# Three stretches of a two-block fp32 network on one Trainium2 core: job order in a recurrent layer, queries and heads in an attention, and a closing norm in columns

## The chip, the cores and the metric

One Trainium2 chip, one core. The metric is the device time of one execution in microseconds (us); the time of a kernel is the median of its runs.

## What is computed

512 tokens of width 1024 go through two layers, then through a third block of another kind and a last norm. Everything is float32. The parts that the change touches, cut from the reference:

```python
def rms_norm(x, g):
    return x * lax.rsqrt(jnp.mean(x * x, axis=-1, keepdims=True) + EPS) * g

def rglru_mixer(h, w_in, conv_w, conv_b, w_a, b_a, w_x, b_x, lam, w_out):   # layer 0
    gate, xr = jnp.split(h @ w_in, 2, axis=-1)
    gate = jax.nn.gelu(gate)
    xc = causal_conv4(xr, conv_w, conv_b)
    r = sigmoid(blockwise(xc, w_a) + b_a)          # 4 blocks of 256
    i = sigmoid(blockwise(xc, w_x) + b_x)
    log_a = -RG_C * r * softplus(-lam)
    u = jnp.sqrt(-jnp.expm1(2 * log_a)) * (i * xc)
    hs = scan(h_t = exp(log_a_t) * h_(t-1) + u_t)
    return (hs * gate) @ w_out

def dsa_mixer(h, w_in, kv_norm_g, w_uk, w_uv, w_o, rel_bias):               # layer 1
    q, c, qi, ki, wi = split(h @ w_in)             # 16 heads of 64, latent 128, 8 index heads
    c = rms_norm(c, kv_norm_g)
    q_lat = einsum('bshd,hdc->bshc', q, w_uk) * ATT_SCALE
    score = einsum('bqh,bqhs->bqs', wi, relu(qi . ki))     # index score, causal
    keep the 256 keys of the highest score for each query
    p = softmax(q_lat . c + rel_bias[t5_bucket(dist)])     # over the kept keys
    o = einsum('bshc,hcv->bshv', p . c, w_uv)
    return o @ w_o

x = x + mixer(rms_norm(x)); x = x + mlp(rms_norm(x))       # each layer
return rms_norm(x, norm_final)                             # after the last block
```

## The kernel before

**Layout and precision.** Activations lie transposed: features on the 128 partitions, the 512 tokens along a row, so a vector of width 1024 is 8 tiles of 128x512. A float32 product is made of three rounded (fp32r) products: both operands are split in a high and a low part, and `group` (lines 349 to 351) issues high by high, high by low and low by high into one PSUM bank. A high part is a copy on ScalarE (`h`, line 362; `wh` for weights, line 252), a low part a subtraction on VectorE (`l`, line 363) or, for weights of some layers, on POOL (`wl`, line 253). Weights come in chunks of 512 KB by SP's DMA queue (`wst`, line 246) in the order of `weight_plan`, with four buffers, three chunks ahead; the copies between tiles stand in the same queue. PSUM has 8 banks, which the pool gives out to one product after the other.

**What sets the order.** The work is written as jobs, lists of stages. `run` pipelines them in software: it starts a job's first stage and then takes a later stage of each of the jobs before it. Every engine works off its queue in order. A scheduler fixes each engine's order once, from the recorded order and priorities.

**Layer 0.** Eight `conv_job`s (projection `xr`, convolution `xc`, lines 541 and 544), four `recur_job`s (weights `ax`; gates `rg` and `ig`, lines 568 and 569; scan, line 598) for 256 features each, and eight `rgate_job`s (projection `rgate`, GELU). The order stands in lines 644 to 651: two projections a step, a recurrence job after each of the steps 2 to 5, and after step 4 `bias_job` (lines 622 to 640): a small product of the 32-row bias table with a one-hot matrix, copied out of PSUM by VectorE (`biasrow`, line 639) and stored to DRAM for the attention. Then come the output projections (`rout`, lines 666 to 668).

**Attention.** `index_job` makes the scores (lines 779 to 798). `select` (lines 811 to 814) finds the 256 best keys: per block of 128 queries 16 rounds of MAX8 and MATCH_REPLACE on VectorE, then the mask; the rounds are handed out in the last stages of `q_job` (four each) and of the first heads (two each). `q_job` projects two heads' queries. `kt_job` makes keys and copies halves of them across partitions by DMA (line 849), `v_job` makes values (lines 870 and 873). For each two heads and each half of the tokens ("pair" 0 and 1), `copies` (line 890) brings the queries into a doubled layout by four DMAs of 64 KB (`qd`), and `queries` rounds the copy: `qph` on ScalarE (line 895), `qpl` on POOL (line 896). `head_job` runs 32 times: bias tile by DMA (line 911), logits (lines 927 to 929), softmax (lines 938 to 946, the last step `probs` on POOL), transposes of the probabilities (line 958), their rounding (`pTh` on ScalarE, line 961, `pTl` on VectorE, line 962), values (lines 978 and 979). The last key block of 128 columns is copied unrounded (`pTf`, line 966) and multiplied in one fp32 product (line 981). After every second head the halves are added (`olo`, lines 985 to 988) and rounded (`oh`, `ol`, lines 993 and 994). The order is lines 1003 to 1022: all projections, then keys, then the first four heads among the values, then the others. Then the output projection `wo`.

**Closing norm.** The last four projections are made in two halves of 256 tokens (`last_job`: residual sum line 1453, square line 1429 or 1427, sum of squares line 1433, weighted output `fin` line 1439). `norm_job` (lines 1460 to 1478) takes the total over features by a product with a matrix of ones, which gives it in all 128 partitions (`tot`, line 1467), then root (1471) and reciprocal (1472) of 128x256, the product with `fin` (1477) and the store (1478). The left half's is put into the job list by line 1514.

Of the kernel before, what the change touches and what calls it, by code (L numbers as in the profile page):

```python
# [222 lines left out]
class Weights:  # L223
# [56 lines left out]
def build(ctx, tc, xT, wall, par, relb, onehot, edges, out):  # L280
# [390 lines left out]
    run([residual_job(j, lambda j=j: rout(j), nxt) for j in range(KD)])  # L671
# [146 lines left out]
    def q_job(j):  # L818
# [60 lines left out]
    QD, QP = {}, {}  # L879
# [4 lines left out]
    def copies(pair, j):  # L884

        t = QD[pair, j] = T(name="qd")
        for f in range(2):
            src = QF[j][64 * f:64 * f + 64, 256 * pair:256 * pair + 256]
            for o in (0, 64):
                nc.sync.dma_start(t[o:o + 64, 256 * f:256 * f + 256], src)  # L890

    def queries(pair, j):
        t = QD.pop((pair, j))
        qh, ql = QP[pair, j] = T(F32R, "qph"), T(F32R, "qpl")
        act(qh, t, AF.Copy)
        G.tensor_sub(ql, t, qh.bitcast(F32))
# [6 lines left out]
    def head_job(pair, h):  # L903
# [44 lines left out]
        def transpose():  # L948
            probs = st["p"]
            st["pT"] = []  # L950
            for k0 in range(0, nfull + 1, 2):
# [7 lines left out]
                nf = 256 if k0 + 1 == nfull else 512  # L959
# [3 lines left out]
                pf = None  # L963
                if nf == 256:
                    pf = T(name="pTf")
                    act(pf[:, :P], ps[:, 256:256 + P], AF.Copy)
                st["pT"].append((ph, pl, pf))

        def values():
# [4 lines left out]
            for kt in range(nfull + 1):  # L974
                ph, pl, pf = st["pT"][kt // 2]
                if kt < nfull:
                    c = slice((kt % 2) * 256, (kt % 2) * 256 + 256)
                    PE.matmul(osl, value(kt, h), ph[:, c], start=kt == 0, stop=False)
                    PE.matmul(osl, value(kt, h), pl[:, c], start=False, stop=False)
                else:  # L980
                    PE.matmul(osl[:, P:], value(kt, h).bitcast(F32), pf[:, :P], start=False, stop=True)
# [568 lines left out]
```

## Time and profile before

| | us |
|---|---|
| median of 3 runs | 1905.25 |
| lowest and highest run | 1904.38, 1905.49 |
| the profiled execution, own time | 1903.61 |
| its span, first to last instruction | 1901.8 |
| TensorE busy | 1848.7 (97%) |
| VectorE busy | 1020.3 (54%) |
| ScalarE busy | 813.4 (43%) |
| POOL busy | 181.7 (10%) |

Times in the rows further down are those of the profiled execution, counted from the start of its span. The engines are named PE (TensorE), PEld (its weight loads), DVE (VectorE), ACT (ScalarE), POOL and SPq (SyncE's DMA queue). Matmuls are pipelined and their ends are modelled; the distance between two starts tells what one costs. "PEclk" is the granted clock of TensorE as a share of its full 2.4 GHz, a mean over the stretch; its other level is 1.2 GHz.

### The profile page before, as it was taken

How to read it: one execution, taken by the hardware profiler on the slowest of the kernel's cores; microseconds unless marked ns; L12 is line 12 of the kernel's file. 1: busy time of each engine (PE TensorE's matmuls, PEld its weight loads, DVE VectorE, ACT ScalarE, POOL GpSimd, SP SyncE). 2: the span in 40 equal slices, each digit the busy share in tenths (PEclk: the TensorE clock that was granted, in tenths of full speed). 3: DMA queues.
4: the chain of work that ended last, by engine and by line, in shares of the span. 5: the costliest groups of instructions: out<-in, count | busy, mean ns of one | idle time of the engine just before them, and what ended most of it. 6: DMA issues, size and time to landing. Idle time of an engine off the chain costs nothing.

```text
span 1901.8 us, 21845 instructions
## 1 busy us (share of the span) xinstructions
PE 1848.7 (97%) x8434; PEld 1526.0 (80%) x8434; DVE 1020.3 (54%) x1512; ACT 813.4 (43%) x1271; POOL 181.7 (10%) x194
## 2 busy tenths in 40 slices
PE   8989999999999679999999999999999999999997
PEld 6868888888878468888888888888888888888886
DVE  7886543344349956654244445735584554344345
ACT  6784432333244577443234445446543333132223
POOL 0000000000155264000000014211000000000000
PEclk9999999999999899999999999999999999999998
DMA  5222222222222530322222222231122222222221
GB/s 197 84 86 92 100 98 91 100 100 96 93 100 90 146 89 21 111 93 96 100 100 92 97 100 86 92 111 45 67 89 100 100 89 100 100 95 94 100 80 53
DMA packets 61000, 179.36 MB, mean 94 GB/s; under 512 B 7696, under 2 KB 18144, under 8 KB 60896
## 3 DMA queue, kind: packets, MB, share of 16 engines
q1 hardware_dynamic: 60752, 177.97, 27.6%
q8 instruction: 66, 1.08, 0.2%
q14 instruction: 38, 0.31, 0.0%
q10 hardware_dynamic: 144, 0.00, 0.0%
HBM read 168.48 MB, written 2.12 MB: 90 GB/s over the span
## 4 chain that ended last, share of the span: by engine, by line
PE 63%; DVE 4%; ACT 2%; issue 1%; DMA 0%; POOL 0%; SPq 0%; DVEq 0%; ACTq 0%
PE ps L349 14%; PE ps L351 13%; PE ps L350 13%; PE dn L350 5%; PE dn L351 5%; PE dn L349 5%; PE o L1319 1%; DVE score L812 1%; PE v L1225 1%; PE v L1224 1%; PE v L1226 1%; DVE top L811 1%; ACT probs L941 1%; PE kv L1293 1%; PE tot L376 0%
## 5 line engine op out<-in xcount | busy, mean ns | idle before, releaser
L252 ACT ACTIVATE wh<-wst 128x1024 fp32r<-128x1024 f32 (+2 forms) x314 | 328.2, 1047 | 910.3 <-PE ps L350 358.7
L349 PE MATMUL ps<-xh,wh 128*128 128x512 f32 x1376 | 542.5, 394 | 6.4 <-DVE biasrow L639 4.6
L351 PE MATMUL ps<-xh,wl 128*128 128x512 f32 x1376 | 536.6, 390 | 0.0
L350 PE MATMUL ps<-xl,wh 128*128 128x512 f32 x1376 | 536.5, 390 | 0.0
L253 DVE TENSOR_TENSOR wl<-wst,wh 128x1024 fp32r<-128x1024 f32 (+2 forms) x291 | 352.4, 1212 | 224.3 <-ACT wh L252 197.2
L349 PEld LDWEIGHTS ps<-xh,wh 128*128 128x128 f32 x1376 | 259.3, 188 | 62.8 <-issue 7.2
L350 PEld LDWEIGHTS ps<-xl,wh 128*128 128x128 f32 x1376 | 259.3, 188 | 56.3 <-issue 2.4
L351 PEld LDWEIGHTS ps<-xh,wl 128*128 128x128 f32 x1376 | 259.1, 188 | 54.1
L349 PE MATMUL dn<-h,wh 128*128 128x512 f32 (+1 forms) x712 | 271.7, 382 | 0.0
L350 PE MATMUL dn<-l,wh 128*128 128x512 f32 (+1 forms) x712 | 271.7, 382 | 0.0
L351 PE MATMUL dn<-h,wl 128*128 128x512 f32 (+1 forms) x712 | 271.7, 382 | 0.0
L350 PEld LDWEIGHTS dn<-l,wh 128*128 128x128 f32 x712 | 133.8, 188 | 26.0
L349 PEld LDWEIGHTS dn<-h,wh 128*128 128x128 f32 x712 | 133.8, 188 | 26.0
L351 PEld LDWEIGHTS dn<-h,wl 128*128 128x128 f32 x712 | 133.8, 188 | 25.8
L253 POOL TENSOR_TENSOR wl<-wst,wh 128x1024 fp32r<-128x1024 f32 x23 | 55.2, 2405 | 934.7 <-ACT wh L252 934.5
L422 DVE TENSOR_TENSOR x<-x,dn 128x512 f32<-128x512 f32 x48 | 33.0, 687 | 170.8 <-PE dn L351 170.8
L453 DVE SCALAR_TENSOR_TENSOR relu<-ps,std 128x512 f32<-128x512 f32 x64 | 44.2, 691 | 146.7 <-PE ps L351 146.6
L349 PE MATMUL ps<-h,wh 128*128 128x512 f32 x200 | 78.7, 396 | 5.5 <-ACT h L362 3.5
L350 PE MATMUL ps<-l,wh 128*128 128x512 f32 x200 | 77.8, 389 | 0.0
L351 PE MATMUL ps<-h,wl 128*128 128x512 f32 x200 | 77.8, 389 | 0.0
L349 PEld LDWEIGHTS ps<-h,wh 128*128 128x128 f32 x200 | 37.9, 190 | 15.1 <-ACT h L362 4.0
L1497 DVE TENSOR_TENSOR u<-ps,std 128x512 f32<-128x512 f32 x22 | 15.2, 690 | 62.5 <-PE ps L351 62.5
(315 smaller groups left out, 2129.2 us busy)
## 6 DMA issues: line engine op xcount, KB each, us to landing
wst<-wall SPq DMA_DIRECT2D x300, 512.0 KB, 3.2
btile<-biasdram SPq DMA_DIRECT2D x32, 128.0 KB, 3.0
qd<-qq SPq DMA_DIRECT2D x64, 64.0 KB, 2.1
wst<-wall SPq DMA_DIRECT2D x8, 384.0 KB, 3.0
x<-xT SPq DMA_DIRECT2D x8, 256.0 KB, 4.9
out_dram<-fin SPq DMA_DIRECT2D x8, 256.0 KB, 2.3
wst<-wall SPq DMA_DIRECT2D x6, 256.0 KB, 5.0
kto<-kth SPq DMA_DIRECT2D x8, 128.0 KB, 2.7
```

The source lines that it names most:

```text
L252: self.nc.scalar.activation(h[:, a:b], st[:, a:b], AF.Copy)
L253: eng.tensor_sub(l[:, a:b], st[:, a:b], h[:, a:b].bitcast(F32))
L349: PE.matmul(ps, wh, xh, start=i == 0, stop=False)
L350: PE.matmul(ps, wh, xl, start=False, stop=False)
L351: PE.matmul(ps, wl, xh, start=False, stop=i == n - 1)
L422: V.tensor_add(xs[j], xs[j], st["ps"])
L453: stt(t, st["ps"], 0.0, feed.r, op0=ALU.max, op1=ALU.mult)
L811: V.max(top, acc[:, :w])
L812: V.match_replace(acc[:, :w], top, acc[:, :w], MARK)
L941: act(s[:, :w], s[:, :w], AF.Exp, scale=-1.0, bias=nm, accum_out=sums[:, a:a + 1])
L1224: PE.matmul(st["ps"][i], xh, hk, start=kt == 0, stop=False)
L1225: PE.matmul(st["ps"][i], xh, lk, start=False, stop=False)
```

## The change

- **Layer 0.** A written list, `LAYER0`, sets the order of the jobs and of the weights: the first recurrence job comes after seven convolutions instead of six, the others among the gate projections. `bias_job` moves from there to the middle of the output projections.
- **Queries.** Each projection's queries are rounded once, whole (`qh` on ScalarE, `ql` on POOL), and both rounded tiles are copied: eight DMAs of 64 KB for two heads and a half, where there were four; the roundings of the copies go. The copies are issued four heads ahead.
- **Order of the attention.** Heads 0 to 7 stand among the last two query projections, the keys 2 to 7 and the values. In the weight plan `uk` and `uv` move ahead of the last two query projections.
- **Weights `wo`.** Their low parts are made on POOL.
- **Values.** The last key block is rounded like the others (`pTh`, `pTl` of 384 columns) and multiplied in two fp32r products; `pTf` goes. `olo` is one copy of 128x512, and the sums go to a tile `os`.
- **Closing norm.** The squares are the weights of the product and one column of ones the moving side, so that the total stands as columns, 128x2; root and reciprocal work on these, and two products with the identity spread the columns over 128x256 in PSUM. The left half's norm starts one job earlier.

```diff
+LAYER0 = ([("xr", j) for j in range(7)] + [("ax", 0), ("xr", 7), ("ax", 1), ("rgate", 0), ("rgate", 1), ("ax", 2)]
+          + [("rgate", 2), ("rgate", 3), ("ax", 3)] + [("rgate", j) for j in range(4, 8)])
 def weight_plan():
-    for step in range(8):
-        plan += [("xr" if step < 4 else "rgate", 2 * step % 8 + i) for i in range(2)]
-        if 2 <= step <= 5:
-            plan += [("ax", step - 2)]
+    plan = list(LAYER0)
-    plan += [("att", j) for j in (0, 1, 2, 3, 4, 6, 7, 8, 9, 5, 10, 11, 12, 13)] + [("uk",), ("uv",)]
+    plan += [("att", j) for j in (0, 1, 2, 3, 4, 6, 7, 8, 9, 5, 10, 11)] + [("uk",), ("uv",), ("att", 12), ("att", 13)]
...
-        eng = self.nc.gpsimd if key[0] in ("att", "uk", "uv", "lr", "k", "dec") or key == ("q", 0) else self.nc.vector
+        eng = self.nc.gpsimd if key[0] in ("att", "uk", "uv", "wo", "lr", "k", "dec") or key == ("q", 0) else self.nc.vector
...
-    for step in range(8):
-        jobs += [(conv_job if step < 4 else rgate_job)(2 * step % 8 + i) for i in range(2)]
-        if 2 <= step <= 5:
-            jobs.append(recur_job(step - 2))
-        if step == 4:
-            jobs.append(bias_job())
+    jobs += [{"xr": conv_job, "ax": recur_job, "rgate": rgate_job}[n](j) for n, j in LAYER0]
...
-    run([residual_job(j, lambda j=j: rout(j), nxt) for j in range(KD)])
+    jobs = [residual_job(j, lambda j=j: rout(j), nxt) for j in range(KD)]
+    run(jobs[:4] + [bias_job()] + jobs[4:])
...
         def ev():
-            t = QF[j] = T(name="qq")
+            t = T(name="qq")
             stt(reverse(t), blocks(st["ps"]), 0.125, blocks(feed.r), op0=ALU.mult, op1=ALU.mult)
+            h, l = QF[j] = T(F32R, "qh"), T(F32R, "ql")
+            act(h, t, AF.Copy)
+            G.tensor_sub(l, t, h.bitcast(F32))
...
     def copies(pair, j):
-        t = QD[pair, j] = T(name="qd")
-        for f in range(2):
-            src = QF[j][64 * f:64 * f + 64, 256 * pair:256 * pair + 256]
-            for o in (0, 64):
-                nc.sync.dma_start(t[o:o + 64, 256 * f:256 * f + 256], src)
-    def queries(pair, j):
-        t = QD.pop((pair, j))
-        qh, ql = QP[pair, j] = T(F32R, "qph"), T(F32R, "qpl")
-        act(qh, t, AF.Copy)
-        G.tensor_sub(ql, t, qh.bitcast(F32))
+        QP[pair, j] = []
+        for src, name in zip(QF[j], ("qph", "qpl")):
+            t = T(F32R, name)
+            for f in range(2):
+                for o in (0, 64):
+                    nc.sync.dma_start(t[o:o + 64, 256 * f:256 * f + 256].bitcast(F32),
+                                      src[64 * f:64 * f + 64, 256 * pair:256 * pair + 256].bitcast(F32))
+            QP[pair, j].append(t)
...
-            n = 8 * pair + j
-            if e == 0 and 1 <= n < 14:
-                copies((n + 2) // 8, (n + 2) % 8)
-            if e == 1 and 1 <= n < 15:
-                queries((n + 1) // 8, (n + 1) % 8)
+            n = 8 * pair + j + 2
+            if e == 0 and n < 16:
+                copies(n // 8, n % 8)
...
-                nf = 256 if k0 + 1 == nfull else 512
+                nf = 384 if k0 + 1 == nfull else 512
...
-                pf = None
-                if nf == 256:
-                    pf = T(name="pTf")
-                    act(pf[:, :P], ps[:, 256:256 + P], AF.Copy)
-                st["pT"].append((ph, pl, pf))
+                st["pT"].append((ph, pl))
...
-                    PE.matmul(osl[:, P:], value(kt, h).bitcast(F32), pf[:, :P], start=False, stop=True)
+                dst = osl if kt < nfull else osl[:, P:]
+                PE.matmul(dst, value(kt, h), ph[:, c], start=kt == 0, stop=False)
+                PE.matmul(dst, value(kt, h), pl[:, c], start=False, stop=kt == nfull)
...
-            act(lo[0:64, :256], ops[64:128, 0:256], AF.Copy)
-            act(lo[64:128, :256], ops[0:64, 256:512], AF.Copy)
+            act(lo, ops, AF.Copy)
+            os_ = T(name="os")
-            V.tensor_add(reverse(lo[0:64, 256:512]), blocks(lo[0:64, :256]), blocks(ops[0:64, 0:256]))
+            V.tensor_add(reverse(os_[0:64, :256]), blocks(lo[64:128, 0:256]), blocks(ops[0:64, 0:256]))
...
-    for j in range(1, 8):
+    for j in range(1, 6):
         jobs.append(q_job(j))
+        if j in (4, 5):
+            jobs.append([lambda: None, lambda j=j: copies(0, j - 4)])
...
-    first = []
-    for i in range(4):
-        first += [heads[i], vals[2 * i], vals[2 * i + 1]]
-    run(jobs + [kt_job(j) for j in range(8)] + first + heads[4:])
+    kts = [kt_job(j) for j in range(8)]
+    jobs += kts[:2] + vals[:2] + [heads[0], q_job(6), heads[1], q_job(7)]
+    for i in range(2, 8):
+        jobs += [heads[i], kts[i], vals[i]]
+    run(jobs + heads[8:])
...
         def tot():
-            ps = st["ps"] = PS("tot")[:, :w]
-            for i in range(2):
-                PE.matmul(ps, ones, acc2[i][:, c], start=i == 0, stop=i == 1)
+            ps = st["ps"] = PS("tot")
+            for n in range(w // P):
+                cols = slice(c.start + n * P, c.start + (n + 1) * P)
+                for i in range(2):
+                    PE.matmul(ps[:, n:n + 1], acc2[i][:, cols], ones[:, 0:1], start=i == 0, stop=i == 1)
         def rstd():
-            r = st["r"] = T(name="std")[:, :w]
-            act(r, st["ps"], AF.Sqrt, scale=1.0 / D, bias=eps_t)
-            V.reciprocal(r, r)
+            col = small(w // P, "rstd")
+            act(col, st["ps"][:, :w // P], AF.Sqrt, scale=1.0 / D, bias=eps_t)
+            V.reciprocal(col, col)
+            st["r"] = PS("r")[:, :w]
+            for n in range(w // P):
+                PE.matmul(st["r"][:, n * P:(n + 1) * P], col[:, n:n + 1].to_broadcast([P, P]), ident, start=True, stop=True)
...
-    jobs.insert(-2, norm_left[:3])
+    jobs.insert(-3, norm_left[:3])
```

What moves on the engines, at three places.

**TensorE in layer 0**, where the high part of the first convolved tile (`h_460`) meets the gate weights of the first recurrence job, in four banks. `ps_435` is the bank of the projection `xr` 5, `ps_530` that of `xr` 6. Before:

```order
L349 MATMUL ps_435<-xh_188,wh_308 128x512
L350 MATMUL ps_435<-xl_189,wh_308 128x512
L351 MATMUL ps_435<-xh_188,wl_309 128x512
L349 MATMUL ps_485<-h_460,wh_340 128x512
L349 MATMUL ps_492<-h_460,wh_340 128x512
L349 MATMUL ps_499<-h_460,wh_340 128x512
L349 MATMUL ps_506<-h_460,wh_340 128x512
L349 MATMUL ps_530<-xh_148,wh_382 128x512
```

Of the change (line numbers one higher; `ps_485` is `xr` 6 here, `ps_572` is `xr` 7):

```order
L350 MATMUL ps_485<-xh_188,wh_340 128x512
L351 MATMUL ps_485<-xl_189,wh_340 128x512
L352 MATMUL ps_485<-xh_188,wl_341 128x512
L350 MATMUL ps_527<-h_460,wh_382 128x512
L350 MATMUL ps_534<-h_460,wh_382 128x512
L350 MATMUL ps_541<-h_460,wh_382 128x512
L350 MATMUL ps_548<-h_460,wh_382 128x512
L350 MATMUL ps_572<-xh_148,wh_430 128x512
```

The same products have moved behind one more projection of 24 matmuls.

**VectorE in the selection**, around the end of the rounds for the second block (384 columns): `wl` are low parts of `wo` chunks, `ktl` and `vv` belong to keys and values, L812 and L811 (L809 and L808 of the change) are the rounds, L814 (L811) the mask. Before:

```order
L826 SCALAR_TENSOR_TENSOR qq<-ps,std 128x4x128
L811 MAX top<-score 128x8 x2
L253 TENSOR_TENSOR wl<-wst,wh 128x1024
L812 MATCH_REPLACE score<-top,score 128x384
L846 TENSOR_TENSOR ktl<-ps,kth 128x512
L812 MATCH_REPLACE score<-top,score 128x512
L846 TENSOR_TENSOR ktl<-ps,kth 128x512 x3
L814 TENSOR_SCALAR mask_3774<-score 128x384
L846 TENSOR_TENSOR ktl<-ps,kth 128x512
L811 MAX top<-score 128x8
L253 TENSOR_TENSOR wl<-wst,wh 128x1024
```

Of the change:

```order
L795 TENSOR_TENSOR score<-score,tri 128x128
L808 MAX top<-score 128x8
L873 TENSOR_TENSOR vv<-ps,vv 128x2x128 x2
L809 MATCH_REPLACE score<-top,score 128x384
L808 MAX top<-score 128x8
L809 MATCH_REPLACE score<-top,score 128x384
L808 MAX top<-score 128x8 x2
L809 MATCH_REPLACE score<-top,score 128x384
L809 MATCH_REPLACE score<-top,score 128x512
L811 TENSOR_SCALAR mask_3774<-score 128x384
L873 TENSOR_TENSOR vv<-ps,vv 128x2x128 x2
```

The `wl` rows are gone from VectorE, the `ktl` rows of the keys 2 to 7 stand further down, and `vv` rows stand here. In front of the last mask there are four `wl`, one `ktl` and four `vv` fewer than before.

**VectorE at the end**, from the last rows of the left half's norm on. Before:

```order
L1433 TENSOR_TENSOR sq<-sq 128x256
L1472 RECIPROCAL std<-std 128x256
L1453 TENSOR_TENSOR x<-x,dn 128x256
L1477 TENSOR_TENSOR fin<-fin,std 128x512 x4
L1433 TENSOR_TENSOR sq<-sq 128x256
L1453 TENSOR_TENSOR x<-x,dn 128x256
L1429 TENSOR_TENSOR sq<-x 128x256
L1472 RECIPROCAL std<-std 128x256
L1477 TENSOR_TENSOR fin<-fin,std 128x512 x4
```

Of the change:

```order
L1421 TENSOR_TENSOR sq<-sq 128x256
L1463 RECIPROCAL rstd<-rstd 128x2
L1441 TENSOR_TENSOR x<-x,dn 128x256
L1471 TENSOR_TENSOR fin<-fin,r 128x512 x4
L1421 TENSOR_TENSOR sq<-sq 128x256
L1441 TENSOR_TENSOR x<-x,dn 128x256
L1421 TENSOR_TENSOR sq<-sq 128x256
L1441 TENSOR_TENSOR x<-x,dn 128x256
L1417 TENSOR_TENSOR sq<-x 128x256
L1463 RECIPROCAL rstd<-rstd 128x2
L1471 TENSOR_TENSOR fin<-fin,r 128x512 x4
```

The left half's four products with `fin` (x4) stand one residual sum and one square earlier, and the reciprocals have two columns.

## Rows read from the trace of the kernel before

**Rows 1.** The page: busy us of each engine, share of the span, instructions.
```profile
PE 1848.7 (97%) x8434; PEld 1526.0 (80%) x8434; DVE 1020.3 (54%) x1512; ACT 813.4 (43%) x1271; POOL 181.7 (10%) x194
```

**Rows 2.** Windows of layer 0: length, busy us of five engines, PEclk, DMA share, GB/s.
```profile
40.00:50.00 10.00, 6.46 (x23) 4.86 (x22) 9.96 (x16) 3.65 (x5) 0.00 (x0) 0.83 0.30 105
80.00:120.00 40.00, 33.84 (x145) 26.38 (x143) 33.34 (x45) 39.37 (x54) 0.00 (x0) 1.00 0.26 90
120.00:140.00 20.00, 19.58 (x80) 16.15 (x81) 16.62 (x24) 16.52 (x22) 0.00 (x0) 0.92 0.24 81
```

**Rows 3.** TensorE's waits in layer 0: releaser, us in total, times, longest.
```profile
PE ps L349 <- DVE biasrow L639: 4.6, 1, 4.6
...
PE ps L349 <- ACT h L362: 3.5, 1, 3.5
```

**Rows 4.** Windows of the attention, columns as in rows 2.
```profile
600.00:660.00 60.00, 44.39 (x197) 34.29 (x196) 58.86 (x144) 28.88 (x71) 21.82 (x22) 0.86 0.48 132
660.00:700.00 40.00, 30.74 (x179) 23.46 (x178) 24.65 (x105) 31.89 (x110) 26.94 (x44) 0.96 0.41 103
700.00:740.00 40.00, 37.66 (x252) 32.92 (x251) 31.30 (x95) 36.22 (x106) 23.16 (x33) 0.96 0.20 44
740.00:760.00 20.00, 19.46 (x103) 16.02 (x103) 7.27 (x17) 8.82 (x25) 4.54 (x7) 1.00 0.00 1
```

**Rows 5.** TensorE's largest wait in the heads.
```profile
PE pT L958 <- POOL probs L946: 9.8, 4, 8.0
```

**Rows 6.** Groups by line and shape, 340 to 762: busy us, mean ns, idle before.
```profile
L253 DVE TENSOR_TENSOR wl<-wst,wh 128x1024 fp32r<-128x1024 f32 x35 | 43.1, 1233 | 27.6 <-ACT wh L252 27.6
...
L253 POOL TENSOR_TENSOR wl<-wst,wh 128x1024 fp32r<-128x1024 f32 x16 | 38.5, 2408 | 554.0 <-ACT wh L252 553.8
...
L896 POOL TENSOR_TENSOR qpl<-qd,qph 128x512 fp32r<-128x512 f32 x16 | 21.4, 1338 | 17.6 <-ACT qph L895 17.6
...
L961 ACT ACTIVATE pTh<-pT 128x256 fp32r<-128x256 f32 x32 | 12.1, 377 | 6.4 <-PE pT L958 6.4
...
L895 ACT ACTIVATE qph<-qd 128x512 fp32r<-128x512 f32 x16 | 10.0, 633 | 0.6 <-PE o L981 0.6
...
L966 ACT ACTIVATE pTf<-pT 128x128 f32<-128x128 f32 x32 | 8.8, 276 | 9.9 <-DVE pTl L962 9.2 <-POOL ol L994 0.6
...
L873 DVE TENSOR_TENSOR vv<-ps,vv 128x256 fp32r<-128x256 f32 x16 | 5.8, 411 | 0.0
...
L846 DVE TENSOR_TENSOR ktl<-ps,kth 128x512 fp32r<-128x512 f32 x8 | 5.3, 676 | 0.0
```

**Rows 7.** SP's issues of copies and bias tiles: ns min/median/max, first and last start.
```profile
L890 SPq DMA_DIRECT2D qd<-qq x64: 462/588/1162, 593.3 to 715.3; - x64
...
L911 SPq DMA_DIRECT2D btile<-biasdram x32: 319/326/1816, 523.9 to 728.6; - x32
```

**Rows 8.** Timeline of TensorE at the values of a head: start, us, instruction.
```profile
725.52 0.28 PE L979 MATMUL o<-pTl,vv 128*128 128x256 f32 x1
725.64 0.38 PE L981 MATMUL o<-pTf,vv 128*128 128x128 f32 x2
```

**Rows 9.** Timeline of the end, and the reciprocal of two columns in the heads.
```profile
1888.54 0.28 PE L351 MATMUL dn<-h,wl 128*128 128x256 f32 x1
1888.73 2.48 DVE L1477 TENSOR_TENSOR fin<-fin,std 128x512 f32<-128x512 f32 x4
...
1891.47 0.41 DVE L1453 TENSOR_TENSOR x<-x,dn 128x256 f32<-128x256 f32 x1
1891.60 2.08 PE L1467 MATMUL tot<-sq,ones 128*128 128x256 f32 x4 [2.78 <-DVE sq L1433]
...
1893.71 0.47 ACT L1471 ACTIVATE std<-tot,eps 128x256 f32<-128x256 f32 x1 [1.30 <-PE tot L1467]
1894.22 1.75 DVE L1472 RECIPROCAL std<-std 128x256 f32<-128x256 f32 x1 [1.88 <-ACT std L1471]
1896.01 2.50 DVE L1477 TENSOR_TENSOR fin<-fin,std 128x512 f32<-128x512 f32 x4
...
L943 DVE RECIPROCAL sums<-sums 128x2 f32<-128x2 f32 x32 | 5.1, 160 | 9.6 <-ACT probs L941 9.6
```

More of the change, by code (lines that the diff above doesn't have):

```diff
@@ L97, in mlp_plan @@
     return plan
+LAYER0 = ([("xr", j) for j in range(7)] + [("ax", 0), ("xr", 7), ("ax", 1), ("rgate", 0), ("rgate", 1), ("ax", 2)]
+          + [("rgate", 2), ("rgate", 3), ("ax", 3)] + [("rgate", j) for j in range(4, 8)])
 def weight_plan():
-    plan = []
-    for step in range(8):
-        plan += [("xr" if step < 4 else "rgate", 2 * step % 8 + i) for i in range(2)]
-        if 2 <= step <= 5:
-            plan += [("ax", step - 2)]
+    plan = list(LAYER0)
     plan += [("routk", kk) for kk in range(4)] + [("rout", j) for j in range(4, 8)]
     plan += mlp_plan(0, HID_GROUPS, False)
-    plan += [("att", j) for j in (0, 1, 2, 3, 4, 6, 7, 8, 9, 5, 10, 11, 12, 13)] + [("uk",), ("uv",)]
+    plan += [("att", j) for j in (0, 1, 2, 3, 4, 6, 7, 8, 9, 5, 10, 11)] + [("uk",), ("uv",), ("att", 12), ("att", 13)]
     plan += [("wo", j) for j in range(8)]
@@ L875, in v_job @@
         return [mm, ev]
-    QD, QP = {}, {}
+    QP = {}
     BT = [T(name="btile") for _ in range(4)]
@@ L974, in values @@
             for kt in range(nfull + 1):
[L975 to L980, printed above, removed]
-                    PE.matmul(osl[:, P:], value(kt, h).bitcast(F32), pf[:, :P], start=False, stop=True)
+                ph, pl = st["pT"][kt // 2]
+                c = slice((kt % 2) * 256, (kt % 2) * 256 + (256 if kt < nfull else P))
+                dst = osl if kt < nfull else osl[:, P:]
+                PE.matmul(dst, value(kt, h), ph[:, c], start=kt == 0, stop=False)
+                PE.matmul(dst, value(kt, h), pl[:, c], start=False, stop=kt == nfull)
             if e == 0:
@@ L984, in values @@
             lo = T(name="olo")
-            act(lo[0:64, :256], ops[64:128, 0:256], AF.Copy)
-            act(lo[64:128, :256], ops[0:64, 256:512], AF.Copy)
-            V.tensor_add(reverse(lo[0:64, 256:512]), blocks(lo[0:64, :256]), blocks(ops[0:64, 0:256]))
-            V.tensor_add(reverse(lo[64:128, 256:512]), blocks(lo[64:128, :256]), blocks(ops[64:128, 256:512]))
+            act(lo, ops, AF.Copy)
+            os_ = T(name="os")
+            V.tensor_add(reverse(os_[0:64, :256]), blocks(lo[64:128, 0:256]), blocks(ops[0:64, 0:256]))
+            V.tensor_add(reverse(os_[64:128, :256]), blocks(lo[0:64, 256:512]), blocks(ops[64:128, 256:512]))
             if pair == 0:
@@ L992, in values @@
             c = slice(256 * pair, 256 * pair + 256)
-            act(oh_[:, c], lo[:, 256:512], AF.Copy)
-            G.tensor_sub(ol_[:, c], lo[:, 256:512], oh_[:, c].bitcast(F32))
+            act(oh_[:, c], os_[:, :256], AF.Copy)
+            G.tensor_sub(ol_[:, c], os_[:, :256], oh_[:, c].bitcast(F32))
         def more():
@@ L1011, in build @@
             jobs += [index_job(2 + (j - 1) // 2, 4 * ((j - 1) % 2) + h) for h in range(4)]
-        if 3 <= j <= 5:
-            jobs.append([lambda: None, lambda j=j: copies(0, j - 3)])
-        if 5 <= j <= 6:
-            jobs.append([lambda: None, lambda j=j: queries(0, j - 5)])
     heads = [head_job(pair, h) for pair in range(2) for h in range(16)]
+    kts = [kt_job(j) for j in range(8)]
     vals = [v_job(kt, n) for kt, n in ((0, 0), (1, 0), (0, 1), (1, 1), (2, 0), (3, 0), (2, 1), (3, 1))]
-    first = []
-    for i in range(4):
-        first += [heads[i], vals[2 * i], vals[2 * i + 1]]
-    run(jobs + [kt_job(j) for j in range(8)] + first + heads[4:])
+    jobs += kts[:2] + vals[:2] + [heads[0], q_job(6), heads[1], q_job(7)]
+    for i in range(2, 8):
+        jobs += [heads[i], kts[i], vals[i]]
+    run(jobs + heads[8:])
     nxt = Feed("g_mlp1")
```

## Prediction

> **What bounds the kernel now.** I read the page first. TensorE is busy for 97% of the span [rows 1], so the kernel can gain only where TensorE waits or runs at its lower clock, or at the end, where the closing chain has no matmul beside it. I then asked windows of the trace for such stretches. Three of them meet this change.
>
> The first is the recurrent layer. From 40 to 50 us TensorE is busy 6.46 of 10 at a mean granted clock of 0.83, and from 120 to 140 the clock is 0.92 [rows 2]: of the two levels, 2.4 and 1.2 GHz, a part ran at the lower, after a wait. The waits of TensorE name the causes [rows 3]: 3.5 us for `h` (line 362: the convolved input of the first recurrence job, rounded too late) and 4.6 us in one piece for `biasrow` (line 639: rgate 6 needs a PSUM bank, and VectorE, in order, has not yet copied the bias product away).
>
> The second is the attention. From 600 to 660 us VectorE is busy 58.86 of 60, while TensorE is busy 44.39 at clock 0.86 [rows 4]. That is the selection: VectorE sets the time. From 660 on, VectorE is no longer full; ScalarE (31.89 of 40) and POOL (26.94) stand in the chain of the heads, and TensorE waits 9.8 us for POOL's `probs`, the largest entry [rows 5]. From 700 on TensorE is nearly full again.
>
> The third is the tail: after the last projection there is a chain of total, root, reciprocal, product and store [rows 9].
>
> **The change, part by part.** Sums are made against the profiled execution, 1903.61 us (span 1901.8).
>
> *Layer 0.* The job `ax0` starts 24 matmuls later, and the bias job stands among the output projections. The two waits are 3.5 + 4.6 = 8.1 us [rows 3]. What the clock lost behind them is (1 - 0.83) x 10 = 1.7 and (1 - 0.92) x 20 = 1.6 us [rows 2], so the most that can go is 11.4. The rest is not free: 24 matmuls at 19.58/80 = 0.245 us [rows 2] put the first gates 5.9 us later in program order, 2.4 beyond the wait that they cover, and ScalarE, 39.37 of 40 busy from 80 to 120, has little room to catch up. I take 11.4 - 2.4 = **9.0 less**; the low end is the bias wait alone, 4.6. The next wait would be at the output projections for the last products of the recurrence. The bias product costs the same in its new place, and its result is first read at 523.9 [rows 7], some 400 us later.
>
> *Selection.* In the order of the change, four low-part splits, one `ktl` and four `vv` subtractions stand no longer before VectorE's last mask: 4 x 1.233 + 0.676 + 4 x 0.411 = 7.25 us [rows 6]. Added there are two sums of halves and one `pTl` (0.41 each, as a `vv` of the same width), and some five `pTl` of 384 columns for 256 (at most half of that more, 0.2; taken at 0.12): 1.85. VectorE is full, so the difference counts: **5.4 less**, between 3 (if VectorE now waits for the late projections in between) and 7.25.
>
> *Heads after the selection.* For two heads ScalarE loses one `qph` (0.633) and two `pTf` (0.276 each), 1.19 us, and gains two `pTh` wider by a half, some 0.25; POOL loses one `qpl`, 1.338 [rows 6]. From 660 to about 745 (ScalarE and POOL are nearly idle from there on [rows 4]) there are 12 sets of two heads, so 5.6 sets in 40 us. In 660 to 700 that is 5.6 x 0.94 = 5.3 by ScalarE and 7.5 by POOL; TensorE idles 9.26 there. I take 6.3. In 700 to 740 TensorE idles 2.34 and loses 1.6 to the clock [rows 4]; not even half of that, 1.7. Together **8.0 less**. Bounds: nothing, and all that TensorE idles or loses from 660 to 760, 9.26 + 2.34 + 0.54 + 2 x 1.6 = 15.3.
>
> *The rounding of whole queries* (8 roundings and 8 subtractions) now stands beside projections, where ScalarE has half its time free (28.88 of 60) and POOL more than that [rows 4]: nothing. If that cover is gone, a late query delays one head by 1.3 us.
>
> *The last key block* as two fp32r products of 128 columns for one fp32 product of two passes. No row shows this form. Nearest is the fp32r product of 256 columns with a pitch of 0.12 us; the fp32 one is 0.38 for two passes, the last of them with its modelled drain [rows 8]. Two products cost between half of the 256-column pitch and all of a drained one more: from -0.06 to +0.2 us a head. Nearest is the same type at its pitch, 2 x 0.12, which is what the two passes take up without the drain; I take **0**, and -2 to +3 for the heads that TensorE bounds. The Trainium skill ("TensorE: Matmul & The Clock Gate", Back-to-back issue gap) gives about 81 ns for a sustained matmul of 128 columns; by it the pair would take 0.16 and the sum would be about 1 us lower (an estimate from that figure). No row here shows a pair of this form, so the sum doesn't use it.
>
> *Copies.* 128 copies of 64 KB for 64: 64 x 0.588 = 37.6 us more of SP's queue, with the bias tiles and the weight chunks for the output projection in line behind them [rows 7]. They are issued four heads ahead, and the issues for two heads take 8 x 0.588 + 2 x 0.326 = 5.4 us, less than the 85 / 12 = 7.1 us of a set now: nothing, and two of the rivals if not.
>
> *`wo` splits on POOL*, 2.408 for 1.233 us [rows 6]. Two stand before the first heads, two in the middle of the first half of the heads, in front of `probs`; POOL is free for most of the selection. The last four stand behind the last `ol`; a chunk's 24 matmuls take 24 x 0.19 = 4.5 us (103 in 19.46 [rows 4]), so POOL keeps ahead: nothing. If the middle two come late, 2 x 2.4 = 4.8 us.
>
> *Closing norm* [rows 9]. The left half's products (2.48 us) now stand before the sum of projection 6 instead of between it and its square, so the last residual sum of the right half, which stands at 1891.47 with its last matmul at 1888.54, no longer waits behind them: it, the last square and the total come up to 2.5 us earlier, and I take 2.1. The reciprocal of 128x256 (1.75) becomes one of 128x2 (0.16): 1.6 less. The root is 0.3 shorter. The total, 2.08 now, becomes eight short passes; between 0.96 at 0.12 each and 2.08, I take 1.3: 0.8 less. Added are two fp32 products of 128 columns, four passes, from 0.5 to 2.1 by the same rows, and I take 1.3 with its hand-over [rows 8]. 2.1 + 1.6 + 0.3 + 0.8 - 1.3 = **3.5 less**, between 1.5 and 4.8.
>
> The sum: 9.0 + 5.4 + 8.0 + 3.5 = 25.9 us, so 1903.61 - 25.9 = 1877.7 for an execution like the profiled one. The median of the runs stands 1.64 us above that one, so the forecast is **1879.4 us**. A measurement of this kernel can tell about 0.2%, 3.8 us, from no change.
>
> **The rivals.**
>
> *TensorE or SP sets the pace of the heads already.* For it: 37.66 of 40 busy from 700 to 740, and 5.4 us of issues for each two heads. Against it: ScalarE and POOL fuller than TensorE from 660 to 700. Then only 17.9 us go: 1887.3. Chance 0.20.
>
> *ScalarE sets the pace of layer 0.* For it: 39.37 of 40 busy between 80 and 120. Then the wait for `h` and its clock loss reappear before the output projections, and 4.6 goes for 9.0: 1883.8. Against it: ScalarE is only 3.65 of 10 busy from 40 to 50 and has free time after 120. Chance 0.12.
>
> *More than I take:* the heads become TensorE-bound throughout, and 15.3 goes for 8.0: 1872.1. For it: both ScalarE and POOL are relieved at once. Against it: each head is still a chain through four engines. Chance 0.12.
>
> *Slower: SP's queue starves the heads.* A copy takes SP 462 to 1162 ns [rows 7]. At 1.16 a set takes 8 x 1.16 + 0.65 = 9.9 us; 16 sets and 24 copies of keys (at the median) are 159 + 14 us from the first copy at 593 on, so the last set is issued at 766. The last heads want it some 12 us before the end of the heads, at 745 - 12 - 13.4 = 720: 46 us late, 1925.4. At the median the same sum ends at 593 + 86 + 14 = 693, 27 us early. It comes out slower than now by over 0.2% from a mean of 1.03 us a copy on, where the last set is 29.7 late. Against it: the median, and that the copies have the same number of bytes as now. Chance 0.05.
>
> **How the numbers follow.** The forecast has 0.51; the rivals have 0.20, 0.12, 0.12 and 0.05. The low end takes the case of 1872.1 with the upper bounds of layer 0 and the norm (2.4 and 1.3) and the gain at the last key block: 1866. The high end takes the first rival with layer 0 at its low bound, 1891.7, and a microsecond for the pair of products: 1893. Faster by over 0.2% (below 1901.4) holds in all cases but the last and its milder forms: 0.94; within 0.2%: 0.02; slower: 0.04.
>
> **What would show it.** Right: no wait of TensorE for `h` around 45 us nor for `biasrow`; VectorE's last mask about 5 us earlier, beyond what layer 0 has gained; sets of two heads at some 6.5 us for 7.1 behind it; the last products starting within 4 us of the last matmul, where now it is 7. Wrong: a wait at the output projections (lines 666 to 668) of more than 3 us; TensorE waiting for the copies of the queries; `probs` late behind two splits of `wo`; VectorE idle before the late queries.

## The result, and the profile after

The change is slower: 1921.84 us, median of 4 runs, against 1904.82 for the kernel before in the same session; ratio 1.0093, interval 1.0075 to 1.0112. The forecast was 1879.4, with 1866 to 1893. The page of the profiled execution (span 1917.7):

```profile
PE 1851.6 (97%) x8450; PEld 1531.4 (80%) x8450; DVE 1020.2 (53%) x1504; ACT 804.2 (42%) x1215; POOL 191.3 (10%) x194
```

TensorE has the same work as before [rows 1] within 3 us, so the loss is waiting. Four marks that both traces have cut the program into stretches: the total of the latent's norm (`csq`), the last mask, the last product of the heads, and the total of the next norm. Before (timeline):

```profile
592.21 1.12 PE L376 MATMUL tot<-csq,ones 128*128 128x512 f32 x2 [1.28 <-ACT csq L756]
662.21 1.43 DVE L814 TENSOR_SCALAR mask<-score 128x512 bf16<-128x512 f32 x1
753.02 0.38 PE L981 MATMUL o<-pTf,vv 128*128 128x128 f32 x2
802.01 0.59 PE L376 MATMUL tot<-sq,ones 128*128 128x512 f32 x1
```

And after:

```profile
586.76 1.13 PE L377 MATMUL tot<-csq,ones 128*128 128x512 f32 x2 [1.28 <-ACT csq L753]
656.47 0.42 DVE L811 TENSOR_SCALAR mask<-score 128x512 bf16<-128x512 f32 x1
770.96 0.27 PE L970 MATMUL o<-pTl,vv 128*128 128x128 f32 x1
821.04 0.59 PE L377 MATMUL tot<-sq,ones 128*128 128x512 f32 x1
```

The stretches between them, in us, with those of the experiments further down:

| kernel | start to csq | csq to mask | mask to last product | to next norm | to the end | median of runs |
|---|---|---|---|---|---|---|
| before | 592.2 | 70.0 | 90.8 | 49.0 | 1099.8 | 1904.8 |
| change | 586.8 | 69.7 | 114.5 | 50.1 | 1096.7 | 1921.8 |
| e4: layer 0 and norm alone | 584.7 | 72.6 | 88.0 | 49.0 | 1096.6 | 1894.4 |
| e12: e4 and the last key block | 584.3 | 74.8 | 84.2 | 45.8 | 1096.6 | 1887.3 |
| e10: e12 with olo and wo | 584.0 | 70.0 | 77.0 | 50.1 | 1096.6 | 1881.7 |
| e1: change, queries rounded late | 584.3 | 75.6 | 73.6 | 50.1 | 1097.1 | 1883.5 |
| e5: e1 with double copies | 585.7 | 74.2 | 101.2 | 50.1 | 1096.7 | 1909.6 |

The start up to `csq` has become 5.4 us shorter and the end 3.1. The stretch from the last mask to the last product has grown by 23.7. The orders differ in how much of the heads stands ahead of the last mask, so the two middle stretches are best read together: from `csq` to the last product it is 160.8 us before, 184.2 in the change, 160.6 in e4, 159.0 in e12, 147.0 in e10, 149.2 in e1 and 175.4 in e5. The windows that answer to [rows 2] and [rows 4]:

```profile
40.00:50.00 10.00, 10.00 (x46) 8.29 (x45) 10.00 (x15) 4.50 (x6) 0.00 (x0) 1.00 0.31 106
50.00:60.00 10.00, 10.00 (x46) 8.28 (x45) 8.79 (x13) 4.69 (x6) 0.00 (x0) 1.00 0.25 88
60.00:70.00 10.00, 5.20 (x14) 3.83 (x14) 6.53 (x10) 7.65 (x11) 0.00 (x0) 0.66 0.18 61
...
120.00:140.00 20.00, 19.88 (x88) 15.94 (x86) 16.26 (x22) 17.02 (x22) 0.00 (x0) 1.00 0.23 82
600.00:660.00 60.00, 45.53 (x200) 35.64 (x198) 55.87 (x154) 27.09 (x70) 25.82 (x29) 0.78 0.54 138
660.00:700.00 40.00, 18.56 (x86) 15.55 (x85) 11.33 (x47) 12.36 (x40) 9.79 (x18) 0.61 0.44 119
700.00:740.00 40.00, 28.98 (x167) 21.96 (x166) 25.45 (x79) 25.71 (x69) 15.25 (x25) 0.96 0.43 104
```

From 660 to 700 every engine is below half: TensorE 18.56 of 40, VectorE 11.33, ScalarE 12.36, POOL 9.79, and TensorE's granted clock is 0.61. No engine is full in that stretch; the work waits for something else. TensorE's longest waits:

```profile
PE o L969 <- ACT pTh L956: 24.8, 8, 14.0
PE ps L350 <- ACT rg L569: 5.3, 2, 4.8
PE pT L953 <- POOL probs L941: 4.8, 3, 3.2
PE logit L924 <- DMA qpl<-ql: 3.6, 2, 3.1
```

The longest, 14.0 us, is for a rounding on ScalarE, and the timeline around it says what ScalarE waited for:

```profile
684.43 2.38 SPq L891 DMA_DIRECT2D qph<-qh  x4
686.86 0.58 SPq L908 DMA_DIRECT2D btile<-biasdram  x1
688.24 2.38 SPq L891 DMA_DIRECT2D qpl<-ql  x4
692.12 0.49 ACT L956 ACTIVATE pTh<-pT 128x384 fp32r<-128x384 f32 x1 [8.37 <-DMA qpl<-ql]
692.66 0.58 PE L969 MATMUL o<-pTh,vv 128*128 128x256 f32 x1 [14.03 <-ACT pTh L956]
```

ScalarE itself waited 8.4 of the 14.0. `pTh` has nothing to do with the copies of queries. It is written into one of the 75 tiles of the pool, and the release names a copy of `ql`: by that, the tile was one of the rounded queries, which comes free when the last copy that reads it has landed. That copy stood in SP's queue, and SP was busy issuing. So two shortages meet: SP's queue and the pool of tiles. The experiments take them apart.

### The profile page after: what moved, and what is told of

The parts are those of the page before. It is cut to its first block, busy times and chain, and to the rows that moved or that the text cites. A ratio compares the mean times of both kernels' runs of the same rounds, so it can differ in the third digit from the quotient of the medians.

```text
span 1917.7 us, 21911 instructions
## 1 busy us (share of the span) xinstructions
PE 1851.6 (97%) x8450; PEld 1531.4 (80%) x8450; DVE 1020.2 (53%) x1504; ACT 804.2 (42%) x1215; POOL 191.3 (10%) x194
## 4 chain that ended last, share of the span: by engine, by line
PE 65%; DVE 2%; DMA 1%; ACT 1%; SPq 1%; issue 1%; POOL 0%; DVEq 0%; ACTq 0%; POOLq 0%
PE ps L350 14%; PE ps L351 14%; PE ps L352 14%; PE dn L350 5%; PE dn L351 5%; PE dn L352 5%; PE o L1307 1%; SPq L891 1%; PE v L1214 1%; PE v L1212 1%; PE v L1213 1%; PE kv L1281 1%; PE pT L953 1%; DMA qpl<-ql 1%; PE o L970 0%
## 5 line engine op out<-in xcount | busy, mean ns | idle before, releaser
L254 DVE TENSOR_TENSOR wl<-wst,wh 128x1024 fp32r<-128x1024 f32 (+2 forms) x283 | 342.7, 1212 | 224.2 <-ACT wh L253 197.3
L254 POOL TENSOR_TENSOR wl<-wst,wh 128x1024 fp32r<-128x1024 f32 x31 | 75.4, 2440 | 918.9 <-ACT wh L253 918.8
L352 PEld LDWEIGHTS dn<-h,wl 128*128 128x128 f32 x712 | 133.8, 188 | 25.9
L969 PE MATMUL o<-pTh,vv 128*128 128x256 f32 x96 | 27.3, 303 | 24.9 <-ACT pTh L956 24.8
```

What stands on the lines that cost most here:

```text
L352: PE.matmul(ps, wl, xh, start=False, stop=i == n - 1)
L969: PE.matmul(dst, value(kt, h), ph[:, c], start=kt == 0, stop=False)
```

## The experiments

Three theories stood at first. S: SP's queue, with 128 copies, is too slow for the heads. T: the sixteen rounded query tiles, held until the second half's copies, leave too few tiles. O: the order, with heads among late keys and values.

**e1, the queries rounded after their copies again.** Everything else of the change stays.

```diff
-            h, l = QF[j] = T(F32R, "qh"), T(F32R, "ql")
-            act(h, t, AF.Copy)
-            G.tensor_sub(l, t, h.bitcast(F32))
+            QF[j] = t
...
+                copies((n + 2) // 8, (n + 2) % 8)
+            if e == 1 and 1 <= n < 15:
+                queries((n + 1) // 8, (n + 1) % 8)
```

> The change with the queries rounded after their copies again (64 copies of one float32 tile, as before); all its other parts stay. Theory S (SP's queue: 128 copies of 0.59 us are too many for the heads): the 24.5 us that the attention lost come back, and some of the forecast gain shows: 1885 to 1897 us. Theory T (75 tiles: sixteen rounded query tiles are held until the second half's copies, and new tiles wait for these reads): the same, 1885 to 1897. Theory O (the order: heads among the late keys and values): no more than 6 us come back, 1915 to 1922.

Measured: 1883.48 us, ratio to before 0.9892 (0.9877 to 0.9906). One part of the change carries 38.4 us of loss; the others together gain 20.7.

**e2, the low parts' copies on ScalarE's queue.**

```diff
-                    nc.sync.dma_start(t[o:o + 64, ...
+                    (nc.sync if name == "qph" else nc.scalar).dma_start(t[o:o + 64, ...
```

> The change with the 64 copies of the low parts issued by ScalarE's DMA queue instead of SP's. Theory S: SP has half the copies, and most of the loss goes, 1890 to 1905 us, less what ScalarE pays for issuing. Theory T: tiles are held as long as in the change, 1915 to 1925. Theory O: 1915 to 1925.

Measured: 1936.63 us (ratio to before 1.0170, 1.0153 to 1.0187), outside all three, 14.8 above the change. In its trace the longest waits for these copies are ScalarE's own (us in total, times):

```profile
  ACT pTh L956: 21.8, 5
  ACT probs L936: 7.8, 3
```

ScalarE now issues the copies in its own order and waits for tiles that they still read. This speaks for T. It does not decide on S, because SP has half the copies but ScalarE has got the other half.

**e3, the order of before**, with the rounded queries and their copies.

```diff
-    for j in range(1, 6):
+    for j in range(1, 8):
         jobs.append(q_job(j))
...
-    jobs += kts[:2] + vals[:2] + [heads[0], q_job(6), heads[1], q_job(7)]
-    for i in range(2, 8):
-        jobs += [heads[i], kts[i], vals[i]]
-    run(jobs + heads[8:])
+    first = []
+    for i in range(4):
+        first += [heads[i], vals[2 * i], vals[2 * i + 1]]
+    run(jobs + [kt_job(j) for j in range(8)] + first + heads[4:])
```

> The change with the order of before in the attention (all query projections, then all keys, then heads; weight plan of before); rounded queries, 128 copies and the other parts stay. Theory S and theory T: still slow, 1910 to 1925 us. Theory O: the loss goes, 1890 to 1897.

Measured: 1917.39 us (1.0070, 1.0055 to 1.0085). Theory O falls: at most 4.4 of the 38.4 us go with the order.

**e4, layer 0 and closing norm alone**, on the kernel before: of the change, these lines and the new `tot` and `rstd`.

```diff
+    plan = list(LAYER0)
+    jobs += [{"xr": conv_job, "ax": recur_job, "rgate": rgate_job}[n](j) for n, j in LAYER0]
+    run(jobs[:4] + [bias_job()] + jobs[4:])
-    jobs.insert(-2, norm_left[:3])
+    jobs.insert(-3, norm_left[:3])
```

> The kernel before with the new order of layer 0, the moved bias product and the closing norm in columns; the attention as before. By the marks in the two traces (first mark 5.4 us earlier, the end 3.1 us shorter) all theories expect 1904.8 - 8.5 = 1896.3 us, within 2 us. If the attention answers to the earlier start in another way, it shows here.

Measured: 1894.38 us (0.9948, 0.9933 to 0.9963). These two parts gain some 10 us by themselves.

**e5, double copies without the tiles.** e1 with every copy made twice, into the tiles of the high and the low part, and rounded there in place:

```diff
+        for name in ("qph", "qpl"):
+            t = T(F32R, name)
...
+    def queries(pair, j):
+        qh, ql = QP[pair, j]
+        act(qh, qh.bitcast(F32), AF.Copy)
+        G.tensor_sub(ql, ql.bitcast(F32), qh.bitcast(F32))
```

> The kernel of e1 (queries kept as one float32 tile, rounded after their copies) with each copy made twice, into the two tiles of the high and the low part, and rounded there in place: 128 copies on SP as in the change, but only 8 query tiles held instead of 16. Theory S (SP's queue): slow again, 1908 to 1922 us. Theory T (tiles held): near e1, 1881 to 1890.

Measured: 1909.59 us (1.0033, 1.0021 to 1.0044), 26.1 above e1, and in the range of theory S. Doubling the copies doubles their bytes too; e9 comes back to that. SP's queue in the timeline (start, us, count at the end):

```profile
676.07 2.38 SPq L888 DMA_DIRECT2D qph<-qq  x4
678.55 2.48 SPq L888 DMA_DIRECT2D qpl<-qq  x4
681.12 1.03 SPq L910 DMA_DIRECT2D btile<-biasdram  x2
682.25 2.38 SPq L888 DMA_DIRECT2D qph<-qq  x4
...
688.49 2.40 SPq L888 DMA_DIRECT2D qph<-qq  x4
...
724.23 2.39 SPq L888 DMA_DIRECT2D qph<-qq  x4
```

At first SP issues here without a pause, one set of two heads every 6.2 us (676.07, 682.25, 688.49). The same eight last sets in e1's queue:

```profile
662.69 2.38 SPq L887 DMA_DIRECT2D qd<-qq  x4
...
666.31 2.38 SPq L887 DMA_DIRECT2D qd<-qq  x4
...
696.74 2.38 SPq L887 DMA_DIRECT2D qd<-qq  x4
```

A set takes 3.6 us there in a row, and later 5.0 to 6.7, when SP waits for the heads. The eighth set from the end is issued 13.4 us later in e5 (676.07 for 662.69). The seven sets behind it take 48.2 us for 34.1, another 14.1. From the last set to the last product it is 36.8 us in both, so nearly all that e5 loses lies ahead of its last set. In its waits ScalarE stands 40.5 us, in ten pieces, for the copies:

```profile
ACT qph L894 <- DMA qph<-qq: 40.5, 10, 7.6
```

**e6, four tiles fewer**, on e1:

```diff
-NT = 75
+NT = 71
```

> The kernel of e1 with 71 tiles of 128x512 in the pool instead of 75: 64 copies, fewer tiles. Theory S: as e1, 1882 to 1887 us. Theory T: half of the eight tiles that the change holds more are missing, so a good part of the 38 us comes back, 1892 to 1920.

Measured: 1888.20 us (0.9918, 0.9903 to 0.9933), 4.7 above e1. Tiles are short, but half of the eight that the change holds more cost 4.7, not the good part of 38 that T alone would need.

**e7, the change with three tiles more**, and three weight staging buffers for four to make room. **e8, e1 with the same.**

```diff
-NT = 75
+NT = 78
...
-        st = pool.tile([P, CHUNK_COLS], F32, name="wst", tag="wst", bufs=4)
+        st = pool.tile([P, CHUNK_COLS], F32, name="wst", tag="wst", bufs=3)
```

> The change with 78 tiles instead of 75 (the weight staging buffers go from four to three for the room). Theory T: three of the eight tiles are given back, 1895 to 1915 us. Theory S: 1917 to 1925, or above if the weights miss their fourth buffer.

> The kernel of e1 with 78 tiles and three staging buffers, beside e7: what the buffer costs by itself. If 75 tiles already limit e1 (theory T), 1876 to 1883 us; by theory S as e1, 1882 to 1886, or above for the missing buffer.

Measured: e7 1911.70 us (1.0040, 1.0025 to 1.0055), 10.1 below the change; e8 1884.37 (0.9897, 0.9883 to 0.9912), as e1 within 1. Three tiles give the change back 10 us and e1 nothing. So of the 38.4 us, 26.1 come with the copies alone (e5). The other 12.3 are a remainder; that they belong to the tiles is supported by the 10.1 that three tiles take back, and no run holds the tiles with all else as in e1.

**e9, the rounded queries laid out by pair.** High and low part of one pair side by side in one tile, four copies of 128 KB for eight of 64 KB; a pair's tile is free after its own copies.

```diff
+            QF[j] = T(F32R, "qhl"), T(F32R, "qhl")
+            for p, hl in enumerate(QF[j]):
+                half = t[:, 256 * p:256 * p + 256]
+                act(hl[:, :256], half, AF.Copy)
+                G.tensor_sub(hl[:, 256:], half, hl[:, :256].bitcast(F32))
...
+            for o in (0, 64):
+                nc.sync.dma_start(t[o:o + 64, :].bitcast(F32), src[64 * f:64 * f + 64, :].bitcast(F32))
```

> The change with the rounded queries laid out by pair: for each pair one tile with high and low part side by side, copied by four DMAs of 128 KB instead of eight of 64 KB; a pair's tile is free after its own copies. 64 copies, and 8 query tiles held after the first half instead of 16; the rounding stays ahead of the copies. Theories S and T together: the loss goes, and the roundings are out of the heads' chain: 1874 to 1884 us (e1: 1883.5). If it is the bytes on the DMA queues and not the number of issues: 1900 or more.

Measured: 1892.32 us (0.9940, 0.9926 to 0.9954), 29.5 below the change with the same bytes copied, though with fewer tiles held in the second half, too. Beside e5, which copies these bytes in twice as many issues, it is 17.3 faster. So the number of issues carries most of e5's loss, and the bytes at most the 8.8 that are left. With 8.8 above e1 it is out of the range that I gave. In the first half sixteen tiles are held here too, and VectorE and POOL wait 4.3 and 3.8 us for tiles that copies still read; whether that is all of the 8.8 was not tried.

**e10, e1 with the old order of the attention.** The lines of e3's diff, on e1, and the calls of `copies` and `queries` where they stood before.

> The kernel of e1 with the attention's order of before (all keys, then heads): what the order is worth without the copies. If the order carries part of e1's gain: 1887 to 1893 us. If the shorter heads (last key block, one olo copy, wo on POOL) carry it: 1881 to 1886.

Measured: 1881.74 us (0.9887, 0.9873 to 0.9901). As e1 within the noise: the new order of the heads is worth nothing here. This is the fastest of the kernels that ran, 22 us under before in its session and 40 under the change.

**e11, e1 with the wo splits on VectorE.**

```diff
-        eng = self.nc.gpsimd if key[0] in ("att", "uk", "uv", "wo", "lr", "k", "dec") or key == ("q", 0) else self.nc.vector
+        eng = self.nc.gpsimd if key[0] in ("att", "uk", "uv", "lr", "k", "dec") or key == ("q", 0) else self.nc.vector
```

> The kernel of e1 with the wo splits on VectorE again: four splits of 1.23 us return to the stretch of the selection. If VectorE bounds that stretch, as the prediction had it: 1886 to 1890 us; if not: 1881 to 1885.

Measured: 1885.29 us (0.9903, 0.9889 to 0.9917), 1.8 above e1, within the noise of the two. The last mask stands 81.3 us behind csq, against 75.6 in e1; but what follows the mask is 3.5 us shorter (70.2 and 73.6). VectorE's work comes through at the mask and mostly not at the end.

**e12, the last key block alone**: e4, with `pTf` gone and two fp32r products of 128 columns.

```diff
-                nf = 256 if k0 + 1 == nfull else 512
+                nf = 384 if k0 + 1 == nfull else 512
...
-                    PE.matmul(osl[:, P:], value(kt, h).bitcast(F32), pf[:, :P], start=False, stop=True)
+                PE.matmul(dst, value(kt, h), ph[:, c], start=kt == 0, stop=False)
+                PE.matmul(dst, value(kt, h), pl[:, c], start=False, stop=kt == nfull)
```

> The kernel of e4 (layer 0 and closing norm new, attention of before) with the last key block rounded like the others, so that pTf goes; olo, wo, order and queries as before. e4 took 1894.4 and e10, with one olo copy and wo on POOL besides, 1881.7. If the pTf copy and what ScalarE waits for in front of it (9.2 us on VectorE's pTl in rows 6) carry the shorter heads: 1883 to 1887 us. If olo and wo carry them: 1890 to 1894.

Measured: 1887.25 us (0.9908, 0.9892 to 0.9925), 7.1 below e4 and a little outside the first range; `olo` and `wo` on POOL, which e10 has besides, are the other 5.5. Both carry a part. The split is rough: e10's four runs lie between 1879.4 and 1884.9, and between the profiled executions the two steps are 5.4 and 8.1.

## Why the prediction was wrong, by its own steps

**Copies: this step failed.** The price of an issue was right: the median is 588 and 594 ns.

```profile
L891 SPq DMA_DIRECT2D qph<-qh x64: 461/588/1605, 597.7 to 736.1; - x64
L891 SPq DMA_DIRECT2D qpl<-ql x64: 461/594/602, 600.2 to 739.3; - x64
```

Two things were wrong in what I compared it with. First, I summed SP's queue freely from its first copy at 593, so that its last set came at 693, 27 us early. But the copies stand in the queue behind the bias tile of their head, and a bias tile waits for a buffer that the softmax of four heads earlier frees: in the change SP stood 10.4 us in three waits for `negmax` (line 933) and 4.6 in four for `sums` (line 938) at the bias tiles. So SP moves on with the heads and can't run ahead. At the last mask 10 of the 16 sets were still to be issued, and the last copy went out at 739.3. Second, I compared 5.4 us of issues with a set of 7.1, the average time of the heads from 660 to 745. SP's own sets stood closer in the kernel before, nine steps in 53.5 us, 5.9 each:

```profile
660.02 2.38 SPq L890 DMA_DIRECT2D qd<-qq  x4
...
713.55 2.39 SPq L890 DMA_DIRECT2D qd<-qq  x4
```

With eight copies a set takes 6.2 in a row, bias tiles and gaps included, and the last sets, relieved of everything else, want 4.9 on average (e1). So 37.6 us more of SP's queue were no "nothing": alone they cost 26.1 us (e5). The rival on SP's queue had the right mechanism and the wrong point: it asked for 1.03 us a copy, and the queue starved the heads at 0.59. The first rival named SP's pace as well, but took it for no gain in the heads, not for a loss.

**Rounding of whole queries: the second failure.** I put it at nothing, and looked for its cover on ScalarE and POOL only. That it holds eight tiles more, out of 75, until the second half's copies has no price in the text at all. The remainder of 12.3 us goes with this step; three tiles more take back 10.1 of it (e7). How much of it the tiles cost and how much the new place of the roundings was not separated.

**Layer 0: 9.0 forecast, 5.4 measured at `csq`.** Both waits are gone, and 40 to 50 and 120 to 140 now run at full clock. In their place stands the largest wait of the layer, 4.80 us for the gates of the first recurrence job, with the lower clock level in the same stretch (a mean of 0.66 in 60 to 70):

```profile
65.70 0.79 PE L350 MATMUL ps<-h,wh 128*128 128x512 f32 x1 [4.80 <-ACT rg L569]
```

The first two recurrence jobs now stand one projection apart, and the second one's banks wait for ScalarE to read the first one's. The rival on ScalarE had nearly the size (4.6), but put the wait at the output projections. At the norm in front of the attention the gain is still 6.6 us, and 5.9 in e4:

```profile
536.23 1.02 PE L376 MATMUL tot<-sq,ones 128*128 128x512 f32 x2
529.64 1.02 PE L377 MATMUL tot<-sq,ones 128*128 128x512 f32 x2
```

The 2 us by which e4, e12, e10 and e1 reach `csq` earlier than the change are lost behind that norm: TensorE waits 2.9 us for `score` in the change and 1.8 in e4, and from 555 to 565 its mean granted clock is 0.83 and 1.00. What makes `score` late was not tried.

**Selection: 5.4 forecast, 0.3 measured.** From the first round of the selection to the last mask it is 95.0 us before and 94.9 in the change. VectorE is busy 92.08 us of the one and 89.42 of the other (the third of the counted figures):

```profile
567.17:662.21 95.04, 77.98 (x350) 61.89 (x349) 92.08 (x236) 43.77 (x96) 32.74 (x29) 0.91 0.40 114
561.55:656.47 94.92, 79.17 (x349) 63.21 (x348) 89.42 (x232) 43.74 (x95) 40.70 (x35) 0.88 0.40 110
```

The rows counted for the forecast did go, but only 2.7 us less work shows, as other instructions took longer, the mask of 256 columns above all (2.06 us for 0.28). And VectorE idles 2.5 us more, most of it before `qq`, where it waits 2.4 us for TensorE's late projections (0.8 before), and before `os` (1.2). "VectorE is full, so the difference counts" failed on these waits, which my low bound of 3 had named, and on the longer instructions, which it had not. e11 shows besides that work on VectorE before the mask moves the mask and less the end: the heads behind the mask take up 3.5 of 5.7 us.

**Heads: without the double copies the direction was right, the cause was not.** I counted the instructions that go: 0.94 us a set on ScalarE, most of it `qph`. e10 keeps `qph` and `qpl` and still shortens mask to last product from 88.0 to 77.0 (e4). What I read past stands in [rows 6]: the `pTf` row shows 8.8 us busy and, behind it, 9.9 us in which ScalarE, in order, waits before that copy, 9.2 of it for VectorE's `pTl`. Taking the copy out takes out both: e12 has no wait of ScalarE for `pTl` left, where e4 has 7.4 us in fifteen. e12 gains 7.1, with its two fp32r products in it.

**Last key block: 0 forecast.** In e10 the pair starts at 716.84 and 716.90 and the next instruction at 717.01:

```profile
716.84 0.23 PE L970 MATMUL o<-pTh,vv 128*128 128x128 f32 x1
716.90 0.27 PE L971 MATMUL o<-pTl,vv 128*128 128x128 f32 x1
717.01 0.30 PE L954 MATMUL pT<-ident,probs 128*128 128x128 f32 x1
```

That is 0.17 us for the pair, whichever instruction follows. The fp32 product before took 0.22 by the distance to the next start where a logit or a transpose follows, and 0.14 to 0.16 where the values of another head do:

```profile
715.82 0.39 PE L981 MATMUL o<-pTf,vv 128*128 128x128 f32 x2
716.04 0.38 PE L927 MATMUL logit<-mask,identb 128*128 128x512 bf16 x1
...
719.40 0.39 PE L981 MATMUL o<-pTf,vv 128*128 128x128 f32 x2
719.56 0.39 PE L978 MATMUL o<-pTh,vv 128*128 128x256 f32 x1
```

A head gains 0.05 us at the one place and loses 0.01 to 0.03 at the other, so the whole is an estimate of at most 32 x 0.05 = 1.6 us of TensorE, inside the range of -2 to +3. The Trainium skill ("TensorE: Matmul & The Clock Gate", Back-to-back issue gap) gives about 81 ns for a sustained matmul of 128 columns, by estimate 0.16 for the pair; the trace agrees, and my row of 256 columns was further off.

**wo on POOL: nothing forecast, 1.8 us of gain** (e11), which the noise could hide. **Closing norm: 3.5 forecast, 3.1 measured**, with the steps near the forecast: the products start 3.4 us after the last matmul, where it was 7.5 [rows 9]. From the last matmul to the end 4.0 us are gained, and 0.8 are lost ahead of it, where TensorE now also makes the left half's `r` (0.71 us).

```profile
1908.40 0.28 PE L352 MATMUL dn<-h,wl 128*128 128x256 f32 x1
...
1909.18 0.42 DVE L1417 TENSOR_TENSOR sq<-x 128x256 f32<-128x256 f32 x1
...
1909.66 0.83 PE L1458 MATMUL tot<-ones,sq 128*128 128x1 f32 x6 [0.75 <-DVE sq L1417]
1910.53 0.26 ACT L1462 ACTIVATE rstd<-tot,eps 128x2 f32<-128x2 f32 x1 [0.84 <-PE tot L1458]
1910.82 0.17 DVE L1463 RECIPROCAL rstd<-rstd 128x2 f32<-128x2 f32 x1 [1.21 <-ACT rstd L1462]
1911.04 0.71 PE L1466 MATMUL r<-ident,rstd 128*128 128x128 f32 x4 [0.55 <-DVE rstd L1463]
1911.79 2.48 DVE L1471 TENSOR_TENSOR fin<-fin,r 128x512 f32<-128x512 f32 x4 [0.80 <-PE r L1466]
```

All parts but the rounding ahead and its copies came to 20.7 us in e1 where I had summed 25.9; the misses in layer 0 and in the selection were made up in part by `pTf`.

## What to carry to other kernels

A queue of transfers is a resource like an engine: ask how many issues stand between two steps of the loop, in a row and with what else stands there, and whether the queue can run ahead or is tied to the loop by a buffer. When a change makes a value earlier, count how long its tiles are held and who gets them next; a wait for a transfer by an instruction that has nothing to do with it can be the sign of a short pool. And of a row in the list of groups, read the idle time before it as well as its busy time: removing an instruction can remove the wait that it holds up its engine for.

## What was not expected of the hardware

A copy of 128 KB takes SP as long to issue as one of 64 KB: 587 ns in e9, 588 before. In the closing norm the products of one column take 0.83 us for six, where the four of 256 columns [rows 9] took 2.08, their wait for the last square included.
